# Block matrices from a lag table in SBUF, and states of both directions written into one array

## The chip, the cores and the metric

One NeuronCore of one Trainium2 chip runs the whole program. The metric is the device time of one execution in microseconds (us); the profile is of one such execution.

## The reference, cut to what matters

A backbone block of two layers works on 256 latent tokens of width 2048, with 256 context tokens. Layer 0 mixes tokens by a bidirectional diagonal state-space layer (S5) with a GLU behind it, layer 1 by pooling; each layer ends with a convolutional feed-forward net. Only S5 matters here. The 2048 channels form 128 groups of 16 channels, each with 64 complex states in each direction:

```
for direction, rev in ((0, False), (1, True)):
    abar, bbar = discretize(lam, log_step, b)          # per group and state
    hc = scan(abar, uc @ bbar, reverse=rev)            # context tokens
    h  = scan(abar, u @ bbar, reverse=rev, h0=end of hc)
    y += Re(h @ c)
out = glu(gelu(y + d * u))
```

Beside it the kernel must compute the adaLN vectors, products of two conditioning vectors with 2048 x 12288 matrices (`ada_w`), which are read from HBM once.

## The kernel before, in words

The 256 tokens are cut into 32 chunks of 8, the context tokens likewise. Within a chunk the recurrence is a matrix: for each group a 128 x 128 block matrix takes 8 tokens x 16 channels to the same. Its entry depends only on the lag between two tokens, so each group needs 15 lags x 16 x 16 numbers. Between chunks there is a recurrence over chunk states. The work is done in two halves h of 64 groups, and each half in 8 units b of 8 groups.

Steps of a unit, by their names in the order written out by hand (ORDER, L33 to 48; the first digit is the half, the second the unit):

- B (`b_ops`): DVE makes powers of a times B for 8 groups, five operations of 1024 columns.
- T (`b_turn`, L587): PE transposes them (16 transposes), ACT copies them to bt; PE multiplies them with C for every lag (lg), ACT copies the result to the lag table L, and POOL adds the diagonal terms. POOL then stores L to DRAM (`scr`, L617).
- S (`s_unit`): PE multiplies bt with the inputs U (chunks of context and tokens), giving pS, the chunk states. Each product takes the whole of U of two neighbouring groups, 128 columns, of which half is used. ACT copies the states in eight pieces of 64 partitions to two arrays: Sc (in the tile X), context chunks, and Sl (in the tile WL), token chunks. The lower 64 partitions hold the forward direction, the upper 64 the backward one, reversed in the copy.
- t (`tree`): DVE reduces the context states, 32 groups at a time, to the state at the start of the tokens. Z (`scan`): DVE runs the recurrence over 32 token chunks, one step after the other.
- L (`m_load`): ACT issues 8 loads that read the stored lag tables of two units back as block rows, Mt. M (`m_turn`): PE transposes these 8 block matrices, ACT copies them to Mm, of which there are three buffers.
- H (`hist`): ACT copies the chunk states of a unit to Hs (two copies of 64 partitions, in the tile QX), and POOL adds a sum to it. C (`c_ops`): DVE makes C times powers, in the array G. Y (`y_unit`): PE multiplies U with the block matrix and Hs with C's powers into y. O (`y_out`): gelu on ACT, transposes, and a split into high and low parts for the GLU.

Between them stand steps F (`feed`): the next load of 1 MB of `ada_w`, issued by SP to one of the tiles st[0] to st[2] in turn (`self.slots`), and its products (gv) with cpad, which hold PE until the load has landed. The steps "-" and "+" take st[2] out of the turn and put it back. k (`columns`) turns finished adaLN vectors into columns ck that DVE needs to modulate U (D).

The tile framework keeps the engines' order as written (`manual_schedule`): each engine works through its own instructions in the order of ORDER, and waits on semaphores where data or a buffer is not ready. PSUM tiles of the tag "tr" have two buffers; pb, lg, pS, pm, pk and pz share them.

After S5, at about 438 us, the dense part begins (`main`): GLU, feed-forward nets and pooling, with weights streamed through st[0] to st[2].

Of the kernel before, what the change touches and what calls it, by code (L numbers as in the profile page):

```python
# [4 lines left out]
F32 = mybir.dt.float32  # L5
# [23 lines left out]
# the order of S5's parts, each by its name in Net.s5 and how many of its steps come in a row  # L29
ORDER = """  # L30
d1*17 d2*39 sc pl ph F sx F*2 d3 b0 p0 b0 p0 b0*3 p0*2 b0*2 qb0 B00*5 F*2 N F*4 d2 s2 u0*2 k0 qo0 T00*2 B02
T00 u1*2 D000 D001 D000 D001 B01*5 b1*7 S00*2 B02*4 F*2 T01*3 qa0 F*2 T02*3 B03*5 F S01*2 B04*5 F T03 F*2
S02*2 N k1 c01 T03*2 D010 D011 D010 D011 B05 S03*2 c00 T04*2 B05*4 B06 F B06 T04 B06*3 F S04*2 t0*2 T05*3  # L33
B07*5 S05*2 c02 F C00*3 c03 T06*3 S06*2 T07*3 F S07 t0*2 S07 C01*3 c04 t0*6 F t1*10 L00 Z0 C02 - L02 lB lc lt
le C02 Z0 lx Z0 C02 Z0 F c05 Z0 b2 Z0*4 b2 F b2 F Z0 F b2 Z0 b2 Z0 F*2 b2 M00 b2 Z0 F Z0 p1 Z0 F p1 Z0 F M01
L04 p1 in Z0 in Z0 M02 F in Z0*3 p1 Z0*8 F Z0*2 F qb1 qa1 H00 H01 Y00*2 M03 H02 L06 F C03*3 c06 k2 Y01 c07 Y01
H03 M04 F*2 C04*3 N k3 D101 D111 D101 Y02*2 H04 C05*3 Y03*2 D100 O0 M05 H05 M06 F C06*3 O0 Y04*2 H06 M07 C07*3
qo1 D100 Y05*2 F H07 O0 Y06*2 B10*5 Y07*2 O1 F B11*5 + T10*2 D111 T10 T11*3 B12*5 S10*2 O1*2 D110*2 B13*5 F
S11 T12*3 B14*4 S12*2 F T13*3 B15*3 S11 B14 F T14*2 B15*2 F S13*2 c10 C10 F C10*2 T14 F B16 T15*3 B16*4 S14*2
c11 t2*2 B17*5 S15*2 c12 t2*6 F t2*2 c13 T16*3 S16*2 T17*3 S17*2 C11*3 c14 F C12 F*2 t3*4 F t3*5 L10 - t3 L12  # L40
Z1 C12 Z1*2 F C12 Z1 c15 Z1*5 F Z1*2 M10 F Z1*4 M11 Z1 L14 Z1 F Z1*2 M12 Z1*2 F Z1 F Z1*3 F*2 Z1*2 F Z1*4 H10
H11 Y10*2 H12 M13 L16 C13*3 c16 Y11*2 H13 M14 Y12 F Y12 H14 M15 C14 C15*2 Y13 C15 Y13 C14*2 c17 O2 H15 M16
C16*2 F C16 Y14*2 H16 O2 M17 F C17*3 Y15*2 F N W*3 H17 h O2 Y16*2 Y17*2 l O3*2 G O3
# [3 lines left out]
class Net:  # L47
# [47 lines left out]
    def exp(self, out, x, t1, t2):  # L95
        """out = exp(x); x is destroyed. One operation at a time, as the next."""
# [30 lines left out]
    def sincos(self, sn, cs, x, j, z, u, v):  # L127
        """x is destroyed."""
# [31 lines left out]
        # u = sin r, v = cos r; quadrant j = 2 m + b0, m = 2 m2 + b1  # L160
# [38 lines left out]
    # (vector, first column, columns) in the order of their use  # L199
# [45 lines left out]
    def finish(self):  # L245
        """The sums of a finished part, to the columns of its vector."""
# [24 lines left out]
    def stream(self):  # L271
# [14 lines left out]
        # where the low parts of the first piece find room before the others  # L286
# [13 lines left out]
    def high(self, p):  # L300
        """High parts of the pieces up to p."""
        while self.highs <= p and self.highs < len(self.pieces):
            w, hi, lo = self.parts(self.highs)
            self.highs += 1
            self.copy(hi, w, WS)

    def ensure(self, p):
        """High and low parts of the pieces up to p; three loads run ahead of them."""
        while self.lows <= p and self.lows < len(self.pieces):
            self.high(self.lows)  # L310
            w, hi, lo = self.parts(self.lows)
# [13 lines left out]
    def half_pair(self, ps, k0):  # L325
        """Two output tiles, half of their inputs."""
# [11 lines left out]
    def glu0(self):  # L338
        """The first half of the first GLU product, while S5 still runs."""
# [4 lines left out]
    def run(self):  # L344
# [5 lines left out]
        with tc.tile_pool(name="const", bufs=1) as cp, tc.tile_pool(name="mst", bufs=1, space=PSUM) as self.mst, tc.manual_schedule():  # L350
# [28 lines left out]
    def s5(self):  # L379
        tc, nc, A = self.tc, self.nc, self.A  # L380
        con, par = self.con, self.par
        with tc.tile_pool(name="s5c", bufs=1) as cp, tc.tile_pool(name="tb", bufs=2) as tb, tc.tile_pool(
            name="small", bufs=1
        ) as self.small, tc.tile_pool(name="s5y", bufs=1, space=PSUM) as pp, tc.tile_pool(name="s5tr", bufs=2, space=PSUM) as ptr, tc.tile_pool(name="dr", bufs=1, space=DRAM) as dr:
            # --- memory
            Sc = self.X.rearrange("p (k r g) -> p k r g", k=32, r=2)
            Sl = self.WL.rearrange("p (k r g) -> p k r g", k=32, r=2)
# [5 lines left out]
            scr = dr.tile([16, P, 240], F32, name="scr")  # L393
# [9 lines left out]
            # --- loads  # L403
# [41 lines left out]
            # --- discretisation  # L445
# [40 lines left out]
            def bbar(h, g0, g1):  # L486
                """Bb: raw (re, im) in planes 1, 2 -> (re - im, re, -im) of Bbar; one operation each."""
# [17 lines left out]
            def powers(h, pw):  # L505
                """Powers 1..8 of abar: planes re, im, re - im, re + im."""
# [31 lines left out]
            def q_a(pw):  # L538
                """Powers 8, 16, .., 128: planes re, im, -im."""
# [14 lines left out]
            # --- state inputs  # L554
# [31 lines left out]
            def b_turn(h, b):  # L586
                """Their transposes, and products with C for every lag."""  # L587
# [20 lines left out]
                L = self.small.tile([P, 15, 16], F32, name=f"L{h}_{b}", tag="L", bufs=2)  # L608
# [8 lines left out]
                nc.gpsimd.dma_start(scr[i], L.rearrange("p s c -> p (s c)"))  # L617

            def s_unit(h, b, Bt):
                bt = Bt.rearrange("p (g r x) -> p g r x", g=8, r=2)  # L620
                for g in range(0, 8, 4):
                    G = b * 8 + g
                    ps = ptr.tile([P, 4, 2, 128], F32, tag="tr", name=f"pS{h}_{b}_{g}")
                    for i in range(4):
                        for r in range(2):
                            self.mm(ps[:, i, r], bt[:, g + i, r], U[:, G + i : G + i + 2].rearrange("p g k -> p (g k)"), True, True)
                    for lo in (0, 64):
                        for k0, n, T, o0 in ((0, 32, Sc, 0), (32, 31, Sl, 1)):
                            c0 = k0 if lo == 0 else k0 + 32 - n
                            src = ps[lo : lo + 64, :, :, c0 : c0 + n]  # L630
                            if lo:
                                src = src[:, :, :, ::-1]
                            self.copy(T[lo : lo + 64, o0 : o0 + n, :, G : G + 4].rearrange("p k r g -> p g r k"), src)
                    yield 1

            # --- recurrences over chunks
# [35 lines left out]
            # --- readout  # L672
# [45 lines left out]
            def y_unit(h, b):  # L718
# [3 lines left out]
                O, M, Hs = o_view(b), Mm[b % 3], Hm[b % 2]  # L722
# [12 lines left out]
            def y_out(J):  # L735
                """gelu, to channel-major high and low parts; in steps."""
# [12 lines left out]
            # --- modulation  # L749
# [11 lines left out]
            def mod_of(h, g0, g1, v):  # L761
                """The place of modulated inputs, and where they come from: the tokens (v = 0) or the context."""
# [4 lines left out]
            def modulate(h, j, v):  # L767
                """On the vector engine, 32 groups at once."""
# [14 lines left out]
            # --- second half  # L783
# [15 lines left out]
            # --- the order of the parts; a part that comes several times goes on where it was  # L799
# [43 lines left out]
            for h in range(2):  # L843
# [8 lines left out]
                for b in range(8):  # L852
# [9 lines left out]
                    ops["L" + n] = lambda h=h, b=b: m_load(h, b)  # L862
# [63 lines left out]
            # --- the other adaLN vectors: loads ahead, and one product at a time  # L926
# [526 lines left out]
```

## Time and profile before

| | |
|---|---|
| time, median of 3 runs | 2118.12 us (2110.8 to 2123.71) |
| span of the profiled execution, first to last instruction | 2114.3 us |
| granted TensorE clock, mean | 0.950 |
| PE busy | 1928.7 us (91%) |
| DVE busy | 1688.5 us (80%) |
| ACT busy | 1012.9 us (48%) |
| POOL busy | 100.7 us (5%) |

The profiled execution's own time, outside the span, isn't told; its span is 3.8 us under the median of the runs. PE is TensorE, PEld its weight loads, DVE VectorE, ACT ScalarE, POOL GpSimd, SP SyncE; ACTq and SPq are DMA issues of these engines. A row of a timeline gives start, length, engine, line of the kernel, instruction, tile written <- tiles read, sizes, and in brackets the idle time ahead of it with what ended it. Rows of like instructions are merged ("x8"). Almost all small operations go through helpers (L53, L71, L75, L83), so the tile's name tells what a row is. A product of 32-bit numbers shows as two MATMUL rows, a transpose as one.

### The profile page before, as it was taken

The numbers are of one execution on the slowest core, as the hardware profiler recorded it, in microseconds if no ns is written. First come the engines' busy times: TensorE is split into PE (matmuls) and PEld (weight loads), VectorE is DVE, ScalarE is ACT, GpSimd is POOL, SyncE is SP. The second block draws the span as 40 slices with busy tenths as digits, with TensorE's granted clock in tenths as the row PEclk, the third lists the DMA queues.
The fourth block names the chain that finished last, engine by engine and source line by source line (L and its number), as shares of the span: only waits on it lengthen the run. The fifth ranks groups of instructions, "written<-read, shape, count | busy, mean of one in ns | idle before, by whom it ended". The sixth has DMA issues, their size and how long they took to land. (4 is left out here: it accounts for less than half of the span.)

```text
span 2114.3 us, 43382 instructions
## 1 busy us (share of the span) xinstructions
PE 1928.7 (91%) x18772; PEld 1649.7 (78%) x18772; DVE 1688.5 (80%) x2208; ACT 1012.9 (48%) x1247; POOL 100.7 (5%) x145
## 2 busy tenths in 40 slices
PE   4973795599989999999999999889999999999996
PEld 2851573378878888888888888568888888888886
DVE  7889788569989999999998888788777776654444
ACT  2550673465546555555544444555555555544441
POOL 0230251100000000000000000000000000000000
PEclk9896797799989999999999999889999999999998
DMA  7659756989946999998999999507767755655652
GB/s 303 261 202 233 189 207 171 215 341 372 361 174 253 354 351 341 333 340 332 344 342 347 359 355 364 204 31 288 250 248 252 249 199 200 201 197 200 206 198 75
DMA packets 95760, 551.94 MB, mean 261 GB/s; under 512 B 10192, under 2 KB 26832, under 8 KB 34640
## 3 DMA queue, kind: packets, MB, share of 16 engines
q1 hardware_dynamic: 74304, 526.06, 68.3%
q10 hardware_dynamic: 17408, 8.39, 3.2%
q0 software_dynamic: 3856, 14.71, 2.1%
q8 instruction: 147, 2.41, 0.5%
q14 instruction: 45, 0.37, 0.1%
HBM read 545.06 MB, written 4.06 MB: 260 GB/s over the span
## 5 line engine op out<-in xcount | busy, mean ns | idle before, releaser
L83 PEld LDWEIGHTS <-WH 128*128 128x128 f16 x9472 | 926.8, 98 | 118.1 <-issue 9.5
L75 ACT ACTIVATE WH<-st 128x2048 f16<-128x2048 f32 (+1 forms) x304 | 566.8, 1865 | 705.1 <-PE pu L83 379.0
L71 DVE SCALAR_TENSOR_TENSOR WL<-st,WH 128x2048 f16<-128x2048 f32 (+1 forms) x303 | 675.9, 2232 | 272.6 <-ACT WH L75 272.0
L83 PE MATMUL pu<-Z,WH 128*128 128x256 f16 x5376 | 881.2, 273 | 0.0
L83 PE MATMUL pu<-Z,WL 128*128 128x256 f16 x2688 | 732.7, 273 | 0.0
L83 PEld LDWEIGHTS <-WL 128*128 128x128 f16 x4720 | 462.4, 98 | 59.5 <-issue 4.2
L83 PE MATMUL pd<-G,WH 128*128 128x256 f16 x2816 | 461.8, 273 | 0.2 <-DVE G L53 0.2
L83 PE MATMUL pd<-G,WL 128*128 128x256 f16 x1408 | 383.8, 273 | 0.0
L71 DVE SCALAR_TENSOR_TENSOR gac<-ra,cpad,gac 128x1024 f32<-128x1024 f32 x128 | 163.8, 1279 | 6.0 <-DMA ra<-ada 4.6
L83 PE MATMUL pg<-Z,WH 128*128 128x256 f16 x960 | 157.5, 273 | 0.0
L71 DVE SCALAR_TENSOR_TENSOR gac<-st,cpad,gac 128x1024 f32<-128x1024 f32 x112 | 143.3, 1280 | 8.3 <-DMA st<-ada 6.9
L71 DVE SCALAR_TENSOR_TENSOR hc<-pu,cvs,hc 128x255 f32<-128x255 f32 x336 | 138.5, 474 | 0.6 <-ACT hc L77 0.6
L83 PE MATMUL pg<-Z,WL 128*128 128x256 f16 x480 | 130.8, 273 | 1.0 <-DVE WL L71 1.0
L83 PE MATMUL gv<-st,cpad 128*32 128x128 f32 (+2 forms) x1024 | 87.3, 476 | 40.6 <-DMA st<-ada 40.5
L77 ACT ACTIVATE hc<-pu,par,cvs 128x256 f32<-128x256 f32 x168 | 84.2, 551 | 7.4 <-DVE G L53 7.4
L83 PEld LDWEIGHTS gv<-st,cpad 128*32 128x32 f32 x1024 | 30.6, 126 | 72.0 <-DMA st<-ada 56.7
L53 DVE TENSOR_TENSOR G<-cb,QO 128x1024 f32<-128x1024 f32 x32 | 38.9, 1250 | 33.9 <-PE y L83 33.9
L53 DVE TENSOR_TENSOR G<-G,q 128x768 f32<-128x768 f32 (+2 forms) x56 | 49.8, 889 | 5.5 <-ACT q L75 3.6
L75 ACT ACTIVATE X<-pS 64x256 f32<-64x256 f32 x64 | 39.5, 618 | 28.6 <-PE pS L83 27.8
L83 PE MATMUL pf<-Z,WH 128*128 128x256 f16 x256 | 46.4, 286 | 5.9 <-ACT Z L75 3.2
L83 PEld LDWEIGHTS pS<-Y,G 128*128 128x128 f32 x384 | 45.0, 195 | 5.5 <-ACT WL L75 1.8
L83 PE MATMUL pS<-Y,G 128*128 128x128 f32 x384 | 47.6, 282 | 0.6 <-ACT WL L75 0.4
(233 smaller groups left out, 1551.8 us busy)
## 6 DMA issues: line engine op xcount, KB each, us to landing
st<-up SPq DMA_DIRECT2D x176, 1024.0 KB, 5.5
st<-ada SPq DMA_DIRECT2D x128, 1024.0 KB, 7.0
ra<-ada SPq DMA_DIRECT2D x64, 1024.0 KB, 7.0
st<-down SPq DMA_DIRECT2D x64, 1024.0 KB, 5.1
st<-glu SPq DMA_DIRECT2D x32, 1024.0 KB, 7.4
st<-down SPq DMA_DIRECT2D x32, 768.0 KB, 5.4
Cz<-cz POOLq DMA_DIRECT2D x16, 256.0 KB, 3.7
X<-scr ACTq DMA_DIRECT2D x32, 128.0 KB, 7.5
```

The costliest lines, as they stand in the source:

```text
L53: self.nc.vector.tensor_tensor(out=out, in0=a, in1=b, op=op)
L71: self.nc.vector.scalar_tensor_tensor(out, a, s, b, op0, op1)
L75: self.nc.scalar.activation(out, a, f, scale=scale)
L77: self.nc.scalar.activation(out, a, f, bias=bias, scale=scale)
L83: self.nc.tensor.matmul(out, l, r, start=start, stop=stop)
```

## The change

- The lag tables of the 8 units of a half stay in SBUF, side by side in st[2] (240 columns each). The store to DRAM, the loads (L) and the tiles Mt go.
- M transposes eight stretches of 128 columns of the unit's lag table, one for each token of a chunk; the copy puts them in the order that Y reads. Mm has five buffers, four of them in X.
- X and WL are now two parts of one tile XW. The states are seen as one array St of 64 chunk places, in which Sc and Sl are stretches.
- S multiplies each group's own 64 columns of U, with the lower and the upper 64 columns of bt apart: the backward direction reads U reversed. One copy of 128 partitions brings all states of the unit into St.
- In ORDER the steps L go. The first "-" stands ahead of T00 (it stood behind the second tree), "+" behind M07 (behind B11), the second "-" ahead of T10 (behind the fourth tree).

```
-            Sc = self.X.rearrange("p (k r g) -> p k r g", k=32, r=2)
-            Sl = self.WL.rearrange("p (k r g) -> p k r g", k=32, r=2)
+            St = self.XW.rearrange("p (k r g) -> p k r g", k=64, r=2)
+            Sc, Sl = St[:, 1:33], St[:, 32:64]
...
+            lag = [self.st[2][:, i * 240 : i * 240 + 240].rearrange("p (s c) -> p s c", c=16) for i in range(8)]
...
-                L = self.small.tile([P, 15, 16], F32, name=f"L{h}_{b}", tag="L", bufs=2)
+                L = lag[b]
...
-                nc.gpsimd.dma_start(scr[i], L.rearrange("p s c -> p (s c)"))
...
-                for g in range(0, 8, 4):
-                    G = b * 8 + g
-                    ps = ptr.tile([P, 4, 2, 128], F32, tag="tr", name=f"pS{h}_{b}_{g}")
-                    for i in range(4):
-                        for r in range(2):
-                            self.mm(ps[:, i, r], bt[:, g + i, r], U[:, G + i : G + i + 2].rearrange("p g k -> p (g k)"), True, True)
-                    for lo in (0, 64):
-                        for k0, n, T, o0 in ((0, 32, Sc, 0), (32, 31, Sl, 1)):
-                            c0 = k0 if lo == 0 else k0 + 32 - n
-                            src = ps[lo : lo + 64, :, :, c0 : c0 + n]
-                            if lo:
-                                src = src[:, :, :, ::-1]
-                            self.copy(T[lo : lo + 64, o0 : o0 + n, :, G : G + 4].rearrange("p k r g -> p g r k"), src)
-                    yield 1
+                ps = ptr.tile([P, 8, 2, 64], F32, tag="tr", name=f"pS{h}_{b}")
+                for g in range(8):
+                    u = U[:, b * 8 + g].rearrange("p (v k) -> p v k", v=2)
+                    for r in range(2):
+                        self.mm(ps[0:64, g, r], bt[:, g, r, 0:64], u, True, True)
+                        self.mm(ps[64:128, g, r], bt[:, g, r, 64:128], u[:, :, ::-1], True, True)
+                    if g == 3:
+                        yield 1
+                self.copy(St[:, 1:64, :, b * 8 : b * 8 + 8].rearrange("p k r g -> p g r k"), ps[:, :, :, 0:63])
...
-            Mt = [m.rearrange("p (g x) -> p g x", g=16) for m in (self.X[:, 0:2048], self.st[2])]
-            Mm = [m.rearrange("p (g x) -> p g x", g=8) for m in (self.X[:, 2048:3072], self.X[:, 3072:4096], e[4][:, 1024:2048])]
+            Mm = [self.X[:, i * 1024 : (i + 1) * 1024] for i in range(4)] + [e[4][:, 1024:2048]]
...
-            def m_load(h, b):
-                """Two units."""
-                d = scr[h * 8 + b : h * 8 + b + 2].rearrange("u (g c) x -> c (u g) x", c=16)
-                for s in range(8):
-                    nc.scalar.dma_start(Mt[b // 2 % 2][16 * s : 16 * s + 16], d[:, :, (7 - s) * 16 : (7 - s) * 16 + 128])
...
-                for g in range(8):
-                    nc.tensor.transpose(ps[:, g], Mt[b // 2 % 2][:, 8 * (b % 2) + g], self.ident)
-                self.copy(Mm[b % 3], ps)
+                L = lag[b].rearrange("p s c -> p (s c)")
+                for t in range(8):
+                    nc.tensor.transpose(ps[:, t], L[:, (7 - t) * 16 : (7 - t) * 16 + 128], self.ident)
+                self.copy(Mm[b % 5].rearrange("p (g t c) -> p t g c", g=8, t=8), ps.rearrange("p t (g c) -> p t g c", g=8))
```

## Rows read from the trace of the kernel before

**Rows 1.** The page's first line.
```profile
span 2114.3 us, 43382 instructions
```

**Rows 2.** Stretches: us, busy by engine (instructions), PE clock, DMA share, GB/s.
```profile
60.00:147.00 87.00, 78.34 (x1257) 66.65 (x1257) 74.06 (x104) 57.79 (x112) 32.09 (x46) 0.93 0.57 208
...
384.00:405.00 21.00, 10.24 (x97) 3.38 (x97) 0.35 (x1) 5.39 (x6) 1.45 (x2) 0.52 0.90 250
...
500.00:525.00 25.00, 25.00 (x234) 21.88 (x232) 24.79 (x22) 13.64 (x19) 0.00 (x0) 1.00 0.99 367
```

**Rows 3.** Timeline of DVE: nine places where it had waited, 95 to 410.
```profile
100.64 4.63 DVE L53 TENSOR_TENSOR Y<-Y,ck 128x1024 f32<-128x1024 f32 x4 [5.05 <-ACT ck L75]
...
147.15 1.23 DVE L53 TENSOR_TENSOR tr<-WH,X 128x1024 f32<-128x1024 f32 x1 [6.95 <-ACT X L75]
...
220.47 2.89 DVE L53 TENSOR_TENSOR G<-cb,QO 128x1024 f32<-128x1024 f32 x2 [4.40 <-PE y L83]
...
237.55 2.36 DVE L53 TENSOR_TENSOR Y<-Y,ck 128x1024 f32<-128x1024 f32 x2 [2.23 <-ACT ck L75]
...
251.74 2.36 DVE L53 TENSOR_TENSOR G<-cb,QO 128x1024 f32<-128x1024 f32 x2 [2.22 <-PE y L83]
...
279.78 1.23 DVE L53 TENSOR_TENSOR Z<-pz,Z 128x1024 f16<-128x1024 f32 x1 [2.95 <-ACT Z L75]
...
303.12 0.29 DVE L53 TENSOR_TENSOR cd<-cb 128x128 f32<-128x128 f32 x1 [2.60 <-DMA cb<-c]
...
337.88 2.36 DVE L53 TENSOR_TENSOR tr<-WH,X 128x1024 f32<-128x1024 f32 x2 [4.03 <-ACT X L75]
...
404.65 2.36 DVE L53 TENSOR_TENSOR G<-cb,QO 128x1024 f32<-128x1024 f32 x2 [21.01 <-PE y L83]
```

**Rows 4.** Timeline of ACT behind the second scan.
```profile
379.67 16.10 ACTq L703 DMA_DIRECT2D X<-scr  x8
395.82 1.02 ACT L75 ACTIVATE G<-pm 128x1024 f32<-128x1024 f32 x1 [23.36 <-DMA X<-scr]
```

**Rows 5.** Groups by shape, 0 to 450: count | busy us, mean ns | idle before.
```profile
L83 PEld LDWEIGHTS pS<-Y,G 128*128 128x128 f32 x384 | 45.0, 195 | 5.5 <-ACT WL L75 1.8 <-ACT G L75 1.8 <-issue 1.2
...
L75 ACT ACTIVATE X<-pS 64x256 f32<-64x256 f32 x64 | 39.5, 618 | 28.6 <-PE pS L83 27.8
...
L75 ACT ACTIVATE QX<-WL 64x512 f32<-64x512 f32 x32 | 35.5, 1109 | 10.4 <-PE y L83 7.4 <-issue 2.4
...
L75 ACT ACTIVATE gz<-y 128x1024 f32<-128x1024 f32 x4 | 4.1, 1024 | 4.5 <-PE y L83 4.5
```

**Rows 6.** Timeline of PE in S5, single rows of it.
```profile
88.75 1.08 PE L83 MATMUL gv<-st,cpad 128*32 128x128 f32 x32
...
93.06 1.07 PE L83 MATMUL gv<-st,cpad 128*32 128x256 f32 x16
...
98.27 1.96 PE L83 MATMUL pk<-gsc,G 128*128 128x16 f32 x16 [0.37 <-ACT WL L75]
...
103.95 3.84 PE L83 MATMUL pS<-Y,Z 128*128 128x128 f32 x32
...
240.53 0.84 PE L83 MATMUL y<-G,QX 128*32 128x128 f32 x24
...
400.43 1.94 PE L83 MATMUL gv<-st,cpad 128*32 128x512 f32 x8 [3.02 <-DMA st<-ada]
...
418.00 1.94 PE L708 MATMUL pm<-con,st 128*128 128x128 f32 x8 [2.39 <-DMA st<-scr]
```

**Rows 7.** Loads of ada_w (L228) issued from 188.7 to 199.
```profile
DMA to landing us min/median/max: 4.7/4.8/5.1
```

**Rows 8.** Loads of ada_w (L228) issued from 85 to 95.
```profile
DMA to landing us min/median/max: 6.9/7.8/8.1
```

**Rows 9.** Timeline of ACT, copies of a unit's lags, first and last of five.
```profile
104.15 0.43 ACT L75 ACTIVATE L<-lg 128x128 f32<-128x128 f32 x2 [0.76 <-PE lg L83]
...
140.48 0.43 ACT L75 ACTIVATE L<-lg 128x128 f32<-128x128 f32 x2 [0.24 <-PE lg L83]
```

More of the change, by code (lines that the diff above doesn't have):

```diff
@@ L30 @@
 ORDER = """
[L31 to L40, printed above, removed]
@@ L41 @@
-Z1 C12 Z1*2 F C12 Z1 c15 Z1*5 F Z1*2 M10 F Z1*4 M11 Z1 L14 Z1 F Z1*2 M12 Z1*2 F Z1 F Z1*3 F*2 Z1*2 F Z1*4 H10
-H11 Y10*2 H12 M13 L16 C13*3 c16 Y11*2 H13 M14 Y12 F Y12 H14 M15 C14 C15*2 Y13 C15 Y13 C14*2 c17 O2 H15 M16
-C16*2 F C16 Y14*2 H16 O2 M17 F C17*3 Y15*2 F N W*3 H17 h O2 Y16*2 Y17*2 l O3*2 G O3
+d1*17 d2*39 sc pl ph F sx F*2 d3 b0 p0 b0 p0 b0*3 p0*2 b0*2 qb0 B00*5 F*2 N F*4 d2 s2 u0*2 k0 qo0 - T00*2 B02 T00 u1*2
+D000 D001 D000 D001 B01*5 b1*7 S00*2 B02*4 F*2 T01*3 qa0 F*2 T02*3 B03*5 F S01*2 B04*5 F T03 F*2 S02*2 N k1 c01 T03*2
@@ new lines @@
+D010 D011 D010 D011 B05 S03*2 c00 T04*2 B05*4 B06 F B06 T04 B06*3 F S04*2 t0*2 T05*3 B07*5 S05*2 c02 F C00*3 c03 T06*3
+S06*2 T07*3 F S07 t0*2 S07 C01*3 c04 t0*6 F t1*10 Z0 C02 lB lc lt le C02 Z0 lx Z0 C02 Z0 F c05 Z0 b2 Z0*4 b2 F b2 F Z0
+F b2 Z0 b2 Z0 F*2 b2 M00 b2 Z0 F Z0 p1 Z0 F p1 Z0 F M01 p1 in Z0 in Z0 M02 F in Z0*3 p1 Z0*8 F Z0*2 F qb1 qa1 H00 H01
+Y00*2 M03 H02 F C03*3 c06 k2 Y01 c07 Y01 H03 M04 F*2 C04*3 N k3 D101 D111 D101 Y02*2 H04 C05*3 Y03*2 D100 O0 M05 H05
+M06 F C06*3 O0 Y04*2 H06 M07 + C07*3 qo1 D100 Y05*2 F H07 O0 Y06*2 B10*5 Y07*2 O1 F B11*5 - T10*2 D111 T10 T11*3 B12*5
@@ new lines @@
+S10*2 O1*2 D110*2 B13*5 F S11 T12*3 B14*4 S12*2 F T13*3 B15*3 S11 B14 F T14*2 B15*2 F S13*2 c10 C10 F C10*2 T14 F B16
+T15*3 B16*4 S14*2 c11 t2*2 B17*5 S15*2 c12 t2*6 F t2*2 c13 T16*3 S16*2 T17*3 S17*2 C11*3 c14 F C12 F*2 t3*4 F t3*5 t3
+Z1 C12 Z1*2 F C12 Z1 c15 Z1*5 F Z1*2 M10 F Z1*4 M11 Z1 Z1 F Z1*2 M12 Z1*2 F Z1 F Z1*3 F*2 Z1*2 F Z1*4 H10 H11 Y10*2 H12
+M13 C13*3 c16 Y11*2 H13 M14 Y12 F Y12 H14 M15 C14 C15*2 Y13 C15 Y13 C14*2 c17 O2 H15 M16 C16*2 F C16 Y14*2 H16 O2 M17 F
+C17*3 Y15*2 F N W*3 H17 h O2 Y16*2 Y17*2 l O3*2 G O3
@@ L357, in run @@
             self.G = cp.tile([P, 12288], F32, name="G")
-            self.X = cp.tile([P, 4096], F32, name="X")
+            self.XW = cp.tile([P, 8192], F32, name="XW")
+            self.X, self.WL = self.XW[:, 0:4096], self.XW[:, 4096:8192]
             self.Y = cp.tile([P, 4160], F32, name="Y")
             self.WH = cp.tile([P, 4096], F32, name="WH")
-            self.WL = cp.tile([P, 4096], F32, name="WL")
             zv = lambda h, j: self.Z[:, h * 2048 + j * 1024 : h * 2048 + (j + 1) * 1024].bitcast(F16).rearrange("p (k t) -> p k t", t=SEQ)
@@ L383, in s5 @@
             name="small", bufs=1
-        ) as self.small, tc.tile_pool(name="s5y", bufs=1, space=PSUM) as pp, tc.tile_pool(name="s5tr", bufs=2, space=PSUM) as ptr, tc.tile_pool(name="dr", bufs=1, space=DRAM) as dr:
-            Sc = self.X.rearrange("p (k r g) -> p k r g", k=32, r=2)
-            Sl = self.WL.rearrange("p (k r g) -> p k r g", k=32, r=2)
+        ) as self.small, tc.tile_pool(name="s5y", bufs=1, space=PSUM) as pp, tc.tile_pool(name="s5tr", bufs=2, space=PSUM) as ptr:
+            St = self.XW.rearrange("p (k r g) -> p k r g", k=64, r=2)
+            Sc, Sl = St[:, 1:33], St[:, 32:64]
             e = [self.G[:, i * 2048 : (i + 1) * 2048] for i in range(6)]
@@ L392, in s5 @@
             TA = self.WH[:, 3072:4032].rearrange("p (k v g) -> p k v g", k=5, v=3)
-            scr = dr.tile([16, P, 240], F32, name="scr")
             QX = cp.tile([P, 3, 8, HG], F32, name="QX")
@@ L721, in y_unit @@
                 y = self.yt[h, b // 4]
-                O, M, Hs = o_view(b), Mm[b % 3], Hm[b % 2]
+                O, M, Hs = o_view(b), Mm[b % 5].rearrange("p (g x) -> p g x", g=8), Hm[b % 2]
                 for gg in range(2):
@@ L861, in s5 @@
                     ops["Y" + n] = lambda h=h, b=b: y_unit(h, b)
-                    ops["L" + n] = lambda h=h, b=b: m_load(h, b)
             live = {}
```

## The prediction

> **What bounds it now.** The page gives one profiled execution of 2114.3 us [rows 1]. The stretches of time come first [rows 2]: from 500 us on PE is busy 25.00 of 25 us, and the change touches nothing there. Ahead of 438 us lies the state-space layer (S5), where no engine is full. In 60:147 DVE works 74.06 of 87 us and PE 78.34, PE much of it waiting on its own buffers; in 384:405 DVE works 0.35 of 21 us while the DMA engines are 90% busy. In S5 a program order written out by hand feeds five in-order queues, and DVE has the work that nothing in the change shortens (discretisation, powers, trees, scan). So the change can give back only what DVE stands idle, and the timeline of DVE is the third view: nine idle times of over 2 us at places that the change reaches [rows 3], 51.4 us in all. The reader is to see who ended each: ACT X (the states), PE y (the readout), ACT ck, a DMA. The two large ones are 21.01 us ahead of 404.65, after the second scan, and 6.95 us ahead of 147.15, ahead of the second tree.
>
> The 21.01 us are explained by ACT's timeline [rows 4]: ACT issues eight loads of the stored lag table from 379.67 and is held for 16.10 us by it; the next copy starts at 395.82, and the history copies that the readout needs stand behind. The scan had ended at 404.65 - 21.01 = 383.64.
>
> **The change, part by part.** *The lag table stays in SBUF.* Sixteen stores from POOL and 64 loads issued by ACT go, with the waits on them. The block matrices are made as before by eight transposes a unit, only from other columns; 128 transposes before and after, so PE pays nothing new. Their copy is 128x1024 as before, 1.02 us in [rows 4], with its write now in runs of 16; a copy that reads in runs of 16, gz, takes 1024 ns for the same size [rows 5], so I take no change. The other end is the strided history copy, 1109 ns for 512 columns [rows 5], 2.2 us for 1024: 1.2 us more a unit, with DVE hiding it in the scans, about 3 us exposed in the two readouts.
>
> What this frees, by DVE's idle times [rows 3]. After the second scan ACT can copy the history at once: two copies of 1.11 us [rows 5], then the first readout product. Before, that took from the end of the last adaLN product, 400.43 + 1.94 = 402.37 [rows 6], to 404.65, so 2.3 us. 2.2 + 2.3 + about 0.5 for POOL's sum leaves a wait of 5 of 21.01: 16 us gained. That needs the adaLN products of this stretch to be done, since PE has them queued ahead of the readout. There are eleven between the last states and the readout, on two slots. A load takes 4.8 us when the stored table isn't being read beside it [rows 7], a product 1.94 [rows 6], so a pair needs 6.74 and each 3.4: 37 us, against 46 us of tree and scan (337.88 to 383.64). They hide. At the 7.8 us that loads took in a crowded stretch [rows 8] it is 4.9 each, 54 us, and 8 of the 16 are lost. So 8 to 18, taken 16.
>
> After the first scan the wait is 4.40 (220.47), ended by the same chain, with DVE's next powers beside it: I take half, 2.2, of 0 to 4.4. The wait on ck at 237.55, 2.23, follows ACT's next issue of loads: 1.5 of it. The 2.22 at 251.74 stands behind a transpose that waits for the stored table: 2.2. In the last stretch the same kind of wait is seen on PE, 2.39 at 418.00 [rows 6]: 2.4, of 0 to 5, as ACT is held there too.
>
> *The states.* A unit of eight groups had 16 products, 32 instructions of 128 weight columns streaming 128, in 3.84 us [rows 6], that is 120 ns each; half of what they wrote was never read. Now there are 32 products, 64 instructions of 64 weight columns streaming 64, the two directions in neighbouring halves of the array. No row shows that shape. From below: readout products in tiles of 32 columns go at 24 in 0.84 us [rows 6], 35 ns, with four tiles side by side streaming 128; per tile and column the new ones stream as much, so 64 x 35 = 2.2 us. From above: pk streams 16 columns only and still takes 16 in 1.96 us [rows 6], 122 ns, so there the 128 weight columns set the price; half of them, 61 ns, give 3.9 us. The shape lies between 32 and 128 columns; I take 3.0.
>
> The eight copies of 64 partitions go; four of them alone fill 39.5 / 16 = 2.5 us of ACT a unit [rows 5], all eight between 2.5 and 5. In their place stands one of 128 partitions and 1008 columns: from 1.02 us (gz) to 2.2 (the strided history copy, 1109 x 1008 / 512). It writes with the same stride as the old ones, 618 ns for 256 that overlap; I take 1.6. So a unit gets 0.8 us shorter on PE and about 2.5 on ACT (0.3 to 4), and since PE's next transposes wait for these copies to free their PSUM buffer, the two add up: 3.3 of the 9.1 us that a unit takes now ((140.48 - 104.15) / 4 [rows 9]). DVE's 6.95 at 147.15 and 4.03 at 337.88 are waits for the last unit of eight; five units run ahead of it after the last place where DVE was level, 5 x 3.3 = 16 us, so both can go. Taken 6.95 and 3.0; at the other end (0.24 a unit) 1 each. The 2.95 at 279.78 waits for an ACT copy that stands behind state products and their copies: all of it. The 2.60 at 303.12 is a load that POOL issues behind a lag table's sum and its store: 1.5.
>
> *The slots.* The lag table takes st[2] from the start of the first half, so adaLN loads have two buffers where they had three (the later "+" comes too late to be used ahead of the next "-"). Queued behind a load's products on PE are the next state products and pk; behind pk, ck on ACT; behind ck, DVE. The place where it bites is DVE's 5.05 at 100.64. The product at 93.06 [rows 6] had its load issued early in the third slot; with two it goes out after the product at 88.75 ends, 89.83, and at 7.8 us [rows 8] lands at 97.6, 4.5 us late. 0.8 us of it come back on PE and about 1.2 on ACT ahead of ck: DVE starts 2.5 later, between 0 and 5.
>
> *One array for both halves of the states* changes no address that anything reads, so I price it at nothing; were its waits coarser than before, that is a rival below.
>
> **Sum.** 16 + 2.2 + 1.5 + 2.2 + 2.4 + 6.95 + 3.0 + 2.95 + 1.5 - 2.5 = 36.2 us of 2114.3: a span of 2078. The median of the three times, 2118.1, lies 3.8 above this span; the same distance gives 2082 us.
>
> **A rule against it.** The weight loads of the old state products are busy 45.0 us over 384 instructions [rows 5], which at 120 ns [rows 6] run for 46 us: load and product overlap on the same rows of the array. The Trainium skill, page "TensorE: Matmul & The Clock Gate", section "Part 3: Packing small matmuls", says that a weight load overlaps a product in flight only when the two use different row groups. The new products all use all rows, so by that rule nothing would overlap; the trace disagrees for the old shape and is silent on the new one. By the rule the sum would be that of the fourth rival.
>
> **Rivals.** First, column tiles cost what their weights cost: 3.9 us or a little more a unit, and the copy 2.2. Units stay near 9 us, the 6.95 and 4.03 stay but for 1 each, half of the 2.95 too: 6 + 2 + 1.5 = 9.5 us less, and 2.5 more late at ck already counted: 2092. For it: pk. Against: the y rows.
>
> Second, loads on two slots become the bound: 8 us less after the second scan and 2.5 more at ck, 2093. For it: PE waits 3.02 us for its load at 400.43 [rows 6], in a stretch with 90% busy DMA engines. Against: there the stored table is read at the same time, which ends.
>
> Third, the change doesn't do what it says: the copies of the block matrices, which write the lower half of the joined array, are made to wait for the scan in its upper half. PE then holds two of them in PSUM and the adaLN products behind the third start after the scan: about 5 products at 3.4 us in the second half, two of them loaded, and 3 in the first, 12 + 5 us less: 2099. Against: G is one array too, and DVE [rows 3] and ACT [rows 4] both write parts of it in the same stretch.
>
> Fourth, slower: state products in half-width tiles don't overlap with their weight loads, so that each instruction keeps its 120 ns: 64 x 0.12 = 7.7 us a unit. That is 3.84 more on PE and about 3 more a unit than the 9.1 of now; thirteen units on the path (five of the first half, eight of the second) lose 39 us, against 16 + 2.2 + 1.5 + 2.2 + 2.4 - 2.5 = 22 that don't depend on it: 17 slower, 2135. It decides from 1.7 us a unit over 9.1, that is state products of about 6.4 us.
>
> **Chances.** The forecast 0.58, first rival 0.18, second 0.10, third 0.05, fourth 0.05, and 0.04 that the sizes cancel to no change. The first two and the third are faster as well. Within 0.5% is 10.6 us, about what a measurement here can tell from no change. Faster 0.90, same 0.05, slower 0.05. All ten terms at their better ends give 48 us, 2070, and DVE's idle times of under 2 us, which I didn't count, could add a few; the first three rivals end by 2102 with a term or two at its worse end. Range 2066 to 2102.
>
> **What would show it.** No DMA issued by ACT; DVE's wait after the second scan near 5 us, and none ahead of the trees; one copy of 1.6 us a unit from pS; 64 state instructions in 3.0 us; ck some 2.5 us later than 100.64; the readout at about 365 us where it began at 402, and 500:525 as full as now. State units of over 5 us, a wait of over 10 us after the second scan, or a dense part that grows would make it wrong.

## The result, and the profile after

The kernel after takes 2083.84 us (median of 4 runs, 2081.14 to 2087.52) against 2118.99 for the one before on the same chip: a ratio of 0.9846, interval 0.9819 to 0.9872. A second comparison gave 0.9857 (0.9841 to 0.9874). The forecast was 2082. The profiled execution took 2082.69 us; the page's first line answers [rows 1], 33.6 us less:

```profile
span 2080.7 us, 44124 instructions
```

No DMA is issued by ACT any more; its queue is gone from the page. As [rows 2] were the way in before, the stretch of the dense part and that of the second scan come first. From 500 us on PE is as full as it was. In the second scan the DMA engines move 286 GB/s at a share of 0.77, where the kernel before moved 213 at 0.93 and then stood at 0.90 through DVE's wait [rows 2]; its row comes first, then two of the kernel after:

```profile
340.00:384.00 44.00, 18.86 (x95) 6.53 (x99) 41.26 (x146) 2.25 (x3) 1.08 (x2) 0.62 0.93 213
```
```profile
500.00:525.00 25.00, 25.00 (x232) 22.40 (x230) 23.78 (x19) 12.33 (x16) 0.00 (x0) 1.00 0.97 367
323.00:368.00 45.00, 24.31 (x124) 6.04 (x120) 42.63 (x147) 3.07 (x3) 3.61 (x2) 0.58 0.77 286
```

DVE's timeline, single rows at the places that answer to [rows 3]:

```profile
102.63 4.65 DVE L52 TENSOR_TENSOR Y<-Y,ck 128x1024 f32<-128x1024 f32 x4 [7.21 <-ACT ck L74]
142.64 2.36 DVE L52 TENSOR_TENSOR tr<-WH,XW 128x1024 f32<-128x1024 f32 x2 [0.42 <-ACT XW L74]
213.13 2.67 DVE L52 TENSOR_TENSOR G<-cb,QO 128x1024 f32<-128x1024 f32 x2 [1.00 <-PE y L82]
220.76 2.36 DVE L52 TENSOR_TENSOR G<-cb,QO 128x1024 f32<-128x1024 f32 x2 [3.33 <-PE y L82]
227.50 2.36 DVE L52 TENSOR_TENSOR Y<-Y,ck 128x1024 f32<-128x1024 f32 x2 [1.30 <-ACT ck L74]
265.14 1.22 DVE L52 TENSOR_TENSOR Z<-pz,Z 128x1024 f16<-128x1024 f32 x1 [0.64 <-ACT Z L74]
283.44 2.38 DVE L52 TENSOR_TENSOR Z<-st,WH 128x1024 f32<-128x1024 f32 x2 [3.28 <-PE lg L82]
291.77 0.29 DVE L52 TENSOR_TENSOR cd<-cb 128x128 f32<-128x128 f32 x1 [2.53 <-DMA cb<-c]
...
372.67 2.83 DVE L52 TENSOR_TENSOR G<-cb,QO 128x1024 f32<-128x1024 f32 x2 [4.45 <-PE y L82]
```

The reader is to compare the bracket of each with its row before: 21.01 became 4.45, 6.95 became 0.42, and one is new, 3.28 for lg at 283.44. The 2.22 ahead of the powers of the first readout's last unit (C07) and the 4.03 ahead of the fourth tree are gone. ACT's row behind the second scan, against [rows 4], and PE's first GLU product, before and after:

```profile
368.05 4.42 ACT L74 ACTIVATE QX<-XW 64x512 f32<-64x512 f32 x4 [22.91 <-DVE XW L52]
```
```profile
437.70 0.38 PE L83 MATMUL pg_sm<-Z,WH 128*128 128x256 f16 x2
```
```profile
402.65 0.38 PE L82 MATMUL pg_sm<-Z,WH 128*128 128x256 f16 x2
```

So S5 ends 35.05 us earlier, and the dense part gives 1.45 of it back (33.6 in the span). The prediction named a dense part that grows as a sign of being wrong; the four runs of this kernel differ by 6.4 us among themselves, so a growth of 1.45 in one execution decides nothing. The states, against [rows 5, 6]: a unit's 64 instructions, and its copy beside the history copy, by groups:

```profile
104.56 2.08 PE L82 MATMUL pS<-Y,Z 128*64 128x64 f32 x64
```
```profile
L74 ACT ACTIVATE QX<-XW 64x512 f32<-64x512 f32 x32 | 35.9, 1121 | 36.1 <-DVE XW L52 30.7 <-PE y L82 4.8
L74 ACT ACTIVATE XW<-pS 128x1008 f32<-128x1008 f32 x16 | 31.2, 1961 | 39.6 <-PE pS L82 39.6
```

### The profile page after: what moved, and what is told of

Its sections match the earlier page's. It is cut to its first block, busy times and chain, and to the rows that moved or that the text cites. A ratio compares the mean times of both kernels' runs of the same rounds, so it can differ in the third digit from the quotient of the medians.

```text
span 2080.7 us, 44124 instructions
## 1 busy us (share of the span) xinstructions
PE 1901.2 (91%) x19284; PEld 1621.9 (78%) x19284; DVE 1689.6 (81%) x2208; ACT 975.6 (47%) x1135; POOL 102.1 (5%) x129
## 5 line engine op out<-in xcount | busy, mean ns | idle before, releaser
L70 DVE SCALAR_TENSOR_TENSOR XW<-st,WH 128x2048 f16<-128x2048 f32 (+1 forms) x303 | 675.9, 2232 | 270.5 <-ACT WH L74 269.9
L82 PE MATMUL pu<-Z,XW 128*128 128x256 f16 x2688 | 732.7, 273 | 0.0
L82 PEld LDWEIGHTS <-XW 128*128 128x128 f16 x4720 | 462.4, 98 | 59.1 <-issue 3.8
L82 PE MATMUL pd<-G,XW 128*128 128x256 f16 x1408 | 383.8, 273 | 0.0
L82 PE MATMUL pg<-Z,XW 128*128 128x256 f16 x480 | 130.8, 273 | 1.0 <-DVE XW L70 1.0
L82 PE MATMUL y<-G,QX 128*32 128x128 f32 x768 | 31.4, 298 | 36.1 <-ACT QX L74 35.2
L82 PEld LDWEIGHTS y<-G,QX 128*32 128x32 f32 x768 | 23.0, 119 | 39.6 <-ACT QX L74 36.6
L74 ACT ACTIVATE QX<-XW 64x512 f32<-64x512 f32 x32 | 35.9, 1121 | 36.1 <-DVE XW L52 30.7
L74 ACT ACTIVATE XW<-pS 128x1008 f32<-128x1008 f32 x16 | 31.2, 1961 | 39.6 <-PE pS L82 39.6
```

The lines of the kernel that those rows point to most:

```text
L70: self.nc.vector.scalar_tensor_tensor(out, a, s, b, op0, op1)
L74: self.nc.scalar.activation(out, a, f, scale=scale)
L82: self.nc.tensor.matmul(out, l, r, start=start, stop=stop)
```

## The experiments: what held the readout for 21 us

The prediction said: ACT, held by its issue of table loads. **ACT freed.**

```
 def m_load(h, b):
...
-    nc.scalar.dma_start(Mt[b // 2 % 2][16 * s : 16 * s + 16], d[:, :, (7 - s) * 16 : (7 - s) * 16 + 128])
+    nc.gpsimd.dma_start(Mt[b // 2 % 2][16 * s : 16 * s + 16], d[:, :, (7 - s) * 16 : (7 - s) * 16 + 128])
```

> The kernel before, with the loads of the stored lag tables issued by POOL instead of ACT; the same bytes move. Theory (the 21.0 us after the second scan come from ACT being held by its issue of loads, with the history copies behind it): ACT copies the history right after the scan and the wait there falls to 5 to 9 us, 12 to 16 us faster, 2103 to 2107. Rival (they come from the traffic: the block matrices or the loads' products ahead of the readout are late, whoever issues): the wait stays at 17 us or more. If POOL is held by its issue as ACT is, its sum on the history is late in the same way, and the wait stays too, with POOL as what ends it.

It was slower: 2127.66 us, ratio 1.0058 (1.0040 to 1.0077). The theory fell. ACT copies the history as soon as the scan ends, and DVE's wait is nearly as long as it was; PE has five adaLN products queued ahead of y, each waiting for its load. Rows of DVE, ACT and PE:

```profile
412.23 2.36 DVE L53 TENSOR_TENSOR G<-cb,QO 128x1024 f32<-128x1024 f32 x2 [20.54 <-PE y L83]
```
```profile
391.53 4.38 ACT L75 ACTIVATE QX<-WL 64x512 f32<-64x512 f32 x4 [7.02 <-DVE WL L53]
```
```profile
385.70 1.58 PE L83 MATMUL gv<-st,cpad 128*32 128x512 f32 x8 [2.25 <-DMA st<-ada]
393.32 1.94 PE L83 MATMUL gv<-st,cpad 128*32 128x512 f32 x8 [6.04 <-DMA st<-ada]
400.89 1.93 PE L83 MATMUL gv<-st,cpad 128*32 128x512 f32 x8 [5.63 <-DMA st<-ada]
403.19 1.93 PE L83 MATMUL gv<-st,cpad 128*32 128x512 f32 x8 [0.37 <-DMA st<-ada]
407.67 1.94 PE L83 MATMUL gv<-st,cpad 128*32 128x512 f32 x8 [2.54 <-DMA st<-ada]
```

The time was lost elsewhere: POOL's other loads came late, and DVE waited 4.53 and 6.75 us for them at 195.69 and 205.66.

**PE freed**, with ACT's issue and then with POOL's:

```
-M12 Z1*2 F Z1 F Z1*3 F*2 Z1*2 F Z1*4 H10
+M12 Z1*13 H10
...
-c16 Y11*2 H13 M14 Y12 F Y12 H14 M15 C14 C15*2 Y13 C15
+c16 Y11*2 F H13 M14 Y12 F Y12 F*2 H14 M15 C14 C15*2 Y13 F C15
```

> The kernel before, with the last five load-and-product steps (F) of the second scan moved behind the start of the second readout; ACT still issues the table loads. Read by DVE's wait after the second scan (21.0 us before). Theory formed from the run with POOL's issue (two holds end at about the same time: ACT's issue, and PE waiting for loads that the tables' traffic makes late; either alone keeps the wait): the wait stays at 16 to 21 us. Rival (PE's products alone are the cause, ACT's hold was never on the path): it falls to 5 to 9.

> Both at once: the table loads issued by POOL, and the last five F of the second scan behind the start of the readout. The tables' bytes still move. Theory (two holds, each enough by itself): DVE's wait after the second scan falls to 5 to 9 us. Rival (a third one, such as the block matrices themselves being late): it stays over 14.

In the first the wait fell to 6.90, so my second theory, that either hold alone keeps it, missed. But its rival, that ACT's hold was never on the path, isn't shown either, since the run eased both: ACT's issue of eight loads shrank to 7.65 us (16.10 in [rows 4]), while the adaLN loads beside it moved 8.54 MB from 340 to 405 us instead of 11.30. In the kernel before, ACT's history copies end at 396.85 + 4.34 = 401.19 and PE's last adaLN product at 402.37 [rows 6]: two holds that end 1.2 us apart. ACT's hold goes with the traffic: once the moved loads run beside the next tables, six issues hold it for 15.03 us. ACT's row of the kernel before, then DVE's and ACT's rows of this run:

```profile
396.85 4.34 ACT L75 ACTIVATE QX<-WL 64x512 f32<-64x512 f32 x4
```
```profile
389.93 2.83 DVE L53 TENSOR_TENSOR G<-cb,QO 128x1024 f32<-128x1024 f32 x2 [6.90 <-PE y L83]
...
414.37 2.52 DVE L53 TENSOR_TENSOR G<-cb,QO 128x1024 f32<-128x1024 f32 x2 [10.03 <-PE y L83]
```
```profile
376.58 7.65 ACTq L703 DMA_DIRECT2D X<-scr  x8
...
393.20 15.03 ACTq L703 DMA_DIRECT2D st<-scr  x6
```

With both freed the wait was 4.45, under the 5 to 9 expected. But neither kernel gained: 2113.82 and 2129.54 us in one run each, beside 2113.13. In the first the moved loads and the next tables made a new wait of 10.03 us at 414.37. Order alone shifts the wait; the traffic that fills the stretch stays.

**Half the bytes**, with the same issues by ACT at the same places:

```
-    nc.scalar.dma_start(Mt[b // 2 % 2][16 * s : 16 * s + 16], d[:, :, (7 - s) * 16 : (7 - s) * 16 + 128])
+    nc.scalar.dma_start(Mt[b // 2 % 2][16 * s : 16 * s + 16, 0:8], d[:, 0:8, (7 - s) * 16 : (7 - s) * 16 + 128])
```

> The kernel before, with each table load reading one unit's groups instead of two: as many issues, by ACT, at the same places, half the bytes (the second unit's block matrices are then those left in memory; only times are read). Theory (the 21 us after the second scan are DMA time: between 340 and 405 the tables' 3.15 MB fill the DMA engines for 37.6% of 65 us, 24.4 us, and the products that PE has queued ahead of the readout wait for loads behind them): half the tables take 12 us less, the wait falls to 8 to 13 us, ACT's issue of eight loads takes 8 us or less instead of 16.1. Rival (the number of loads and their issue sets it, not their bytes): wait of 18 us or more, issue of 14 or more.

The wait fell to 5.15, further than the 8 to 13 expected, ACT's issue to 9.56 (8 or less expected), and the whole took 2088.95 us in one run beside 2116.16: 27 us less.

```profile
377.92 2.36 DVE L53 TENSOR_TENSOR G<-cb,QO 128x1024 f32<-128x1024 f32 x2 [5.15 <-PE y L83]
```

Both holds shrank with the bytes: ACT's issue ends at 364.29, ahead of the scan's end, and PE's last adaLN product at 375.94, 3.2 us behind it. The DMA view shows why, by queue (packets, MB, share of 16 engines; q1 carries the adaLN loads, q10 the tables). First the kernel before, 340 to 405 us, with 24 table loads; then this one in the 65 us from 330, which begins as far ahead of its scan's end and holds all 32 loads of the half, each of half the size:

```profile
q1 hardware_dynamic: 1555, 11.30, 53.3%
q10 hardware_dynamic: 6528, 3.15, 37.6%
```
```profile
q1 hardware_dynamic: 1871, 13.62, 59.1%
q10 hardware_dynamic: 4608, 2.10, 16.2%
```

The tables went in packets of 3.15 MB / 6528 = 482 bytes on average (they are read in runs of 512). These were under way for 0.376 x 65 = 24.4 us of all sixteen engines, 7.8 us a MB, where an adaLN load took 34.6 / 11.30 = 3.07. With the loads halved a MB of tables costs 0.162 x 65 / 2.10 = 5.0 us and one of adaLN 2.82: the prices hold for a crowded stretch and not for a load alone. That the size of the packets makes the price isn't shown. The run halves bytes and packets alike, and with POOL's issue the loads went in far fewer packets, at a price near 0.312 x 65 / 3.53 = 5.7 us a MB. The queue of POOL's loads in that run, 340 to 405 us, a few others among them:

```profile
q0 software_dynamic: 1296, 3.53, 31.2%
```

The Trainium skill, page "DMA: Bandwidth & Descriptors", section "Issuing engines are not separate DMA queues", says that loads end on the same sixteen engines whoever starts them; the run with POOL's issue agrees, with 20.54 us of wait left of 21.01 when POOL issued them.

## The experiments: the parts of the change by themselves

**Tables in SBUF, states as before.** The kernel after with the old `s_unit`.

> The kernel after, with the state products and their eight copies a unit as before: the lag tables stay in SBUF, two slots for the loads, no stores and no loads of tables. Theory (the gains of the two parts stand beside each other and add up): DVE's wait after the second scan falls from 21.0 to about 5 us, the waits of 2 to 4.7 us in the first readout go in part, ck comes some 2.5 us late, and the waits ahead of the trees (6.95 and 4.03 us) stay: 21 to 25 us faster than before, 2094 to 2098. Rival (the parts need each other: with old state units the two-slot loads and the states fill the stretch, so the loads' products still hold PE after the scan): wait after the second scan over 10 us, gain under 14 us, 2105 or more.

2097.58 us, 0.9916 (0.9897 to 0.9934), 17.8 us less by the ratio. The wait after the scan is 4.44, as in the full change, so here this part needs nothing of the other. The total falls short of the 21 to 25: ck is 5.4 us late (100.64 before), and the fourth tree waits 6.28 where it waited 4.03:

```profile
106.06 4.65 DVE L52 TENSOR_TENSOR Y<-Y,ck 128x1024 f32<-128x1024 f32 x4 [8.09 <-ACT ck L74]
```
```profile
334.74 2.36 DVE L52 TENSOR_TENSOR tr<-WH,XW 128x1024 f32<-128x1024 f32 x2 [6.28 <-ACT XW L74]
...
384.97 2.84 DVE L52 TENSOR_TENSOR G<-cb,QO 128x1024 f32<-128x1024 f32 x2 [4.44 <-PE y L82]
```

**Slots alone.** In ORDER of the kernel before, "-" ahead of T00, "+" behind M07, "-" ahead of T10; the two "-" and the "+" of before go:

```
-k0 qo0 T00*2
+k0 qo0 - T00*2
...
-M07 C07*3
+M07 + C07*3
...
-F B11*5 + T10*2
+F B11*5 - T10*2
```

> The kernel before with nothing but the steps that take the third slot out of the turn, and put it back, where the change has them. Theory: ck and with it DVE's modulation in the first half come 2 to 2.5 us late, nothing else on the path moves: 1 to 4 us slower, 2120 to 2123. Rival (two slots make the loads of the scans the bound): the waits after both scans grow, 8 us or more slower, 2127 or more.

2123.05 us, 1.0040 (1.0019 to 1.0061): 8.5 us slower by the ratio (4.0 to 12.9), the rival's size at the theory's place. DVE's first modulation, and PE ahead of it:

```profile
109.59 4.65 DVE L53 TENSOR_TENSOR Y<-Y,ck 128x1024 f32<-128x1024 f32 x4 [11.99 <-ACT ck L75]
```
```profile
99.45 1.93 PE L83 MATMUL gv<-st,cpad 128*32 128x256 f32 x16 [3.10 <-DMA st<-ada]
101.31 5.85 PE L83 MATMUL pS<-Y,Z 128*128 128x128 f32 x32
```

ck is 8.95 late. The load for the product at 99.45 is issued at 93.14 where it was 85.11, and the product starts 6.4 us after its old place at 93.06 [rows 6]; 3.2 of these had been lost ahead of that load, whose forerunner's product runs at 91.99 for 88.75. Then PE runs its next work slowly: 1.93 and 5.85 us, where [rows 6] have 1.07 and 3.84 for the same shapes. The wait after the second scan hardly grew (22.63). That says little of two slots there, since the kernel before had taken st[2] out of the turn for both scans too; the landing times in the section on the prediction decide it.

**States alone.** The kernel before with XW, St and the new `s_unit`.

> The kernel before, with the states made by own products into one array and by one copy a unit; the lag tables still go through DRAM, the loads still have three slots. Theory: the waits of 6.95 us ahead of the second tree and 4.03 ahead of the fourth go, 2.95 at 279.78 in part, and the 21 us after the second scan stay: 9 to 13 us faster, 2106 to 2110. Rival (one array makes false waits: the table loads into its lower half have to wait for the scan in its upper half): ACT's issue of loads moves from inside the scan to its end, and the wait after the second scan grows to 25 us or more: no gain, or slower, 2115 to 2135.

2106.24 us, 0.9968 (0.9950 to 0.9986): 6.8 us less by the ratio, under the 9 to 13 expected, with an interval up to 10.6. The 4.03 ahead of the fourth tree is gone, the 6.95 became 3.39; waits of the first readout and for cb grew (4.18 at 245.79, 4.41 at 300.05). The wait after the second scan, expected to stay at 21, is 13.74. The rival, false waits in the joined array, fell: the scan ended at 390.38 - 13.74 = 376.64, and ACT began to issue loads into the array's lower half ten us ahead of that:

```profile
366.85 14.97 ACTq L699 DMA_DIRECT2D XW<-scr  x8
```
```profile
390.38 2.36 DVE L53 TENSOR_TENSOR G<-cb,QO 128x1024 f32<-128x1024 f32 x2 [13.74 <-PE y L83]
```

The two parts give 17.8 + 6.8 = 24.6 us, the whole 30.2 (26.6 to 33.6) in the second comparison and 32.6 (27.1 to 38.4) in the first. The sum's own uncertainty is some 5 us, so an interplay of the parts is not shown by the times; in the traces there is one: with the shorter states ck comes at 102.63 instead of 106.06.

## The experiments: what sets the states' price

> The kernel after, with the state products of four groups in another order: eight of the lower half of the array, then eight of the upper, where the change alternates them. Theory (a unit's 64 instructions take 2.08 us because instructions of neighbouring halves run beside each other): in this order they take 3 to 3.9 us, 48 to 61 ns each. Rival (half the weight columns and half the streamed columns halve the price whatever comes next): 2.1 to 2.2 us as before.

```
-for g in range(8):
-    for r in range(2):
-        self.mm(ps[0:64, g, r], bt[:, g, r, 0:64], u, True, True)
-        self.mm(ps[64:128, g, r], bt[:, g, r, 64:128], u[:, :, ::-1], True, True)
+for g0 in (0, 4):
+    for lo in (0, 64):
+        for g in range(g0, g0 + 4):
...
+            for r in range(2):
+                self.mm(ps[lo : lo + 64, g, r], bt[:, g, r, lo : lo + 64], u[:, :, ::-1] if lo else u, True, True)
```

```profile
101.88 3.41 PE L82 MATMUL pS<-Y,Z 128*64 128x64 f32 x64
```

3.41 us, in all of the five units of 100 to 140 us, against 2.08: 53 ns and 32.5 ns an instruction. (In the kernel after three of the five take 2.08 or 2.09, one 2.49, and one is broken by a stop shown at the end.) The order of the halves is worth 1.3 us a unit, so instructions in neighbouring halves do run beside each other; whether it is the products or a weight load beside a product, the run doesn't tell. One run took 2086.71 us.

> The kernel after, with the copy of a unit's states written to one stretch of 1008 columns of the array, so that the states are not where the scan looks for them; only the copy's duration is read. Theory (the copy's 1.96 us come from its write in steps of 512 bytes): 1.0 to 1.1 us. Rival (from its read in runs of 63, or from its four-level pattern): 1.9 to 2.0 us still.

```
-self.copy(St[:, 1:64, :, b * 8 : b * 8 + 8].rearrange("p k r g -> p g r k"), ps[:, :, :, 0:63])
+self.copy(self.XW[:, 128 + b * 1008 : 1136 + b * 1008].rearrange("p (g r k) -> p g r k", g=8, r=2), ps[:, :, :, 0:63])
```

```profile
L74 ACT ACTIVATE XW<-pS 128x1008 f32<-128x1008 f32 x16 | 16.2, 1012 | 36.1 <-PE pS L82 36.1
```

1012 ns against 1961: the write in steps of 512 bytes doubles the copy, 1.95 ns a column instead of 1.0. The Trainium skill, page "SBUF — State Buffer", section "Door 1: The DMA port swizzle", says that accesses which each cross to another 16-byte line pay a penalty; these rows agree, and put it at (1961 - 1012) / 1008 = 0.94 ns an element for this one step.

## The experiments: the waits that the change left

S11's two halves of products stand apart in ORDER. Before, each had a PSUM tile of its own; now one tile covers both and is held from 264.31 to its copy behind 284, so that T12 and T13 have one "tr" buffer. PE's rows:

```profile
264.31 1.15 PE L82 MATMUL pS<-Y,G 128*64 128x64 f32 x32 [0.16 <-ACT XW L74]
...
280.24 1.09 PE L592 MATMUL pb<-con,Z 128*128 128x128 f32 x8 [1.11 <-ACT G L74]
282.44 1.16 PE L82 MATMUL lg<-Z,Cz 64*32 64x128 f32 x64 [1.11 <-ACT G L74]
283.53 1.15 PE L82 MATMUL pS<-Y,G 128*64 128x64 f32 x32
```

That makes the 3.28 at 283.44. As to the 7.21 at 102.63: PE runs a product of the next part at 95.96, having waited 2.68 for its load, ahead of k1, which doesn't need it. Four steps moved, then a fifth:

```
-T03 F*2 S02*2 N k1 c01
+T03 F S02*2 N k1 F c01
...
-c06 k2 Y01 c07 Y01
+c06 Y01 c07 Y01 k2
...
-T10 T11*3
+T10 c10 T11*3
...
-S11 T12*3
+S11*2 T12*3
...
-B15*3 S11 B14
+B15*3 B14
...
-S13*2 c10 C10
+S13*2 C10
```

and for the fifth:

```
-T03 F S02*2 N k1 F c01
+T03 F N S02*2 k1 F c01
```

> The kernel after, with four steps moved in the order: the first load's products of the next part (F) behind k1 instead of ahead of it; k2 behind the second Y01; the two halves of S11 together; the load c10 ahead of T11. Theory (each of these waits of DVE after the change is ended by the queued step that I named): ck comes 3 to 4.5 us earlier (wait of 7.21 us at 102.63 falls to 3 to 4), the 3.33 at 220.76, the 3.28 at 283.44 and the 2.53 at 291.77 fall under 1 each: 9 to 12 us faster than after, 2069 to 2074 where after is 2082. Rival (PE or the loads are late anyway, the waits only move): under 4 us faster than after, 2078 or more.

> The kernel after, unchanged, beside the one before it on the same chip: 2080 to 2086.

> The kernel with the four moved steps, and a fifth: the sums of the finished part (N) ahead of S02 instead of behind it, so that ACT copies their row before the states of S02. Theory: POOL's sum is no longer behind that copy, ck comes 3 to 5 us earlier still (first modulation of the second quarter at 98 to 100, 103.09 with four): 2072 to 2075 where four moved steps gave 2077. Rival (the load that lands at 91.3 or the first tree behind it sets the time anyway): 2076 or more.

Four steps: 2077.39 us, 0.9830 (0.9816 to 0.9845), where after had 2082.87 in the same comparison: 5.5 less, between theory and rival. The 3.33, the 2.53 and the 3.28 went (a wait of 1.15 for lg stands at a later place), but ck came only at 103.09: DVE had a new wait of 4.16 ahead of it, for POOL's sum, whose row ACT copies behind S02's states. The fifth step takes that away:

```profile
98.55 4.63 DVE L52 TENSOR_TENSOR Y<-Y,ck 128x1024 f32<-128x1024 f32 x4 [2.42 <-ACT ck L74]
...
286.48 2.38 DVE L52 TENSOR_TENSOR G<-st,WH 128x1024 f32<-128x1024 f32 x2 [1.09 <-PE lg L82]
```

2073.09 us, 0.9803 (0.9784 to 0.9822), within the 2072 to 2075 expected. It beats the kernel before; against after it was measured on another chip, and its interval is clear of after's second one (0.9841 to 0.9874) and just touches the first (0.9819 to 0.9872).

## Why the prediction was right, point by point

The forecast of 2082 met 2083.84, and DVE's idle times account for it place by place (us; forecast and measured):

| term | forecast | measured |
|---|---|---|
| wait after the second scan, 21.01 to 4.45 | 16 | 16.6 |
| readout 1: 4.40 to 1.00 (and 4.71 to 3.33, not counted) | 2.2 | 3.4 (+1.4) |
| ck at 237.55, 2.23 to 1.30 | 1.5 | 0.9 |
| 2.22 at 251.74, gone | 2.2 | 2.2 |
| from the first readout wait of half 2 to the GLU, 33.05 to 29.98 | 2.4 | 3.1 |
| second tree, 6.95 to 0.42 | 6.95 | 6.5 |
| fourth tree, 4.03 to none | 3.0 | 4.0 |
| 2.95 to 0.64 | 2.95 | 2.3 |
| cb, 2.60 to 2.53 | 1.5 | 0.1 |
| ck at 100.64, 5.05 to 7.21 | -2.5 | -2.2 |
| lg at 283.44 | none | -3.3 |
| sum | 36.2 | 35.0 |

That the sum came within 1.2 is in part luck: the places that gave more than forecast make 5.2 us, those that gave less, cb and lg above all, 6.4. One of the former, the 4.71 at 229.70 in the kernel before, was missing from the prediction's nine idle times of over 2 us.

**The largest term had the right size with half of the cause.** "The 21.01 us are explained by ACT's timeline": not by it alone. With ACT free the wait was 20.54; with half the tables' bytes, 5.15. PE's queue was late by the tables' traffic, 24.4 us of DMA time, and ACT's hold was the same congestion, seen on another engine. The estimate held because the change takes away the bytes, and with them both holds, and because its size came from the chain that is left behind the scan: 5 us forecast, 4.45 measured. Its condition, that the adaLN products of the scan hide on two slots, was right, though there are thirteen behind the last states and not eleven: the loads issued from 318 to 352 us landed as fast as those in [rows 7], and the last product was done at 360.22, eight ahead of the scan's end at 372.67 - 4.45 = 368.22. Their line, from issue to landing:

```profile
DMA to landing us min/median/max: 4.7/4.8/5.4
```

**Two sizes of the states were off, in opposite ways.** The products take 2.08 us where I took 3.0, just under the lower end of 2.2 from the y rows; the copy takes 1.96 where I took 1.6 of 1.02 to 2.2. Of "3.3 of the 9.1 us" a unit only 9.08 - 7.28 = 1.8 shows (st<-lg copies on ACT at 104.59 and 119.15); over the same four units as before it is (137.69 - 104.59) / 4 = 8.28, a stop of PE of 3.44 us among them that no wait explains (last section). It was enough to end both tree waits.

**The slots' price was mis-sized.** "DVE starts 2.5 later, between 0 and 5" was worked out from one load; by itself the edit makes ck 8.95 late and the kernel 8.5 us slower. With the tables kept in SBUF 5.4 remain, and with the shorter states, in the whole change, 2.0.

**One mechanism was missing.** The prediction has no term for the joined PSUM tile of a unit; where its halves are issued apart it holds one of two buffers for 20 us, 3.3 us on the path. And cb's 2.60 had nothing to do with POOL's store: moving its issue ended it.

**The rivals.** Column tiles at the price of their weights (3.9 us), and no overlap (7.7), fell: 2.08 alternated, 3.41 apart. By the rule of the Trainium skill weighed in the prediction ("TensorE: Matmul & The Clock Gate", "Part 3: Packing small matmuls") nothing would overlap on the same rows; the traces disagree, for the old shape and both orders of the new: over the 768 instructions of the same tiles, weight loads are busy 25.0 us and products 26.9 in the kernel after, 40.8 and 42.5 with the halves apart, at 35 and 55 ns an instruction, so in both they lie over each other. Loads as the bound fell with the scans' loads, false waits with the run of the states alone.

## What to carry to other kernels

An engine held by its DMA issues can be a symptom: before blaming it, look at what the DMA engines are filled with in that stretch and which queue the waiting engine itself is behind. Loads in short runs can cost DMA time far beyond their bytes (here 3.15 MB read in runs of 512 bytes took as long as 8 MB of large loads), and the time was gained by not moving them, not by moving their issue. When two PSUM tiles become one, check that nothing is issued between its halves.

## What the runs showed of the hardware that I had not expected

Instructions on the two column halves of the array overlap when they alternate: 32.5 ns each, against 53 ns when one half's eight come in a row.

A late load can cost more than its lateness. In the kernel with the slots alone PE sat idle for 3.10 us ahead of 99.45; over that stretch the granted clock was 0.72 on average, between the two levels of 1.2 and 2.4 GHz, where the kernel before had 1.00 for the same products. That the idle time lowered it isn't shown: the kernel before has 0.57 in the 4 us behind that, with no such gap ahead. The row of the slots alone, then two of the kernel before:

```profile
96.00:108.00 12.00, 8.81 (x57) 7.34 (x57) 0.44 (x4) 3.01 (x7) 1.95 (x5) 0.72 0.76 285
```
```profile
92.00:100.00 8.00, 6.89 (x66) 6.10 (x66) 3.59 (x7) 4.67 (x11) 1.98 (x3) 1.00 0.95 362
100.00:104.00 4.00, 3.87 (x76) 3.24 (x75) 3.36 (x3) 1.61 (x3) 0.00 (x0) 0.57 0.24 98
```

In the kernel after PE stops inside a unit's states, behind 27 of the 64 instructions, for 3.44 us without any wait that the profile shows. The run with the halves apart has no such stop in that stretch; the cause stays open.

```profile
125.88 1.03 PE L82 MATMUL pS<-Y,Z 128*64 128x64 f32 x27
130.36 2.19 PE L82 MATMUL pS<-Y,Z 128*64 128x64 f32 x37 [3.44 <-issue]
```
